# Buffer pairs re-laid and taken in another order, x and ctx loaded over 128 partitions, two transposes ahead of a copy

## The chip, the core and the metric

The kernel runs on one core of a Trainium2 chip. The metric is the device time of one execution in microseconds (us); the text gives the median of several. TensorE is called PE, VectorE DVE, ScalarE ACT, GpSimd POOL. SP is the engine whose queue issues nearly all loads here. It issues them one after the other: a load whose buffer is not yet free holds up every load behind it.

## The reference

One layer of a diffusion transformer: 512 latent tokens and 256 context tokens of 1024 numbers each.

```python
h = modulate(rms_norm(x, p['norm_pre_mix']), sh_m, sc_m)       # shift and scale come from c @ w_ada
u, q, k, v, ga, gb = split_in(h @ p['w_in'])                    # and the same for ctx
ya = s5_mixer(uc, u, p)                                         # state-space branch, scan over the tokens
yb = diff_attention(q, concat(kc, k), concat(vc, v), ...)
x  = x + g_m * rms_norm(merge_branches(ya, yb, ga, gb, p), p['norm_post_mix'])   # ends in "@ p['w_out']"
h  = modulate(rms_norm(x, p['norm_pre_ffn']), sh_f, sc_f)
...
aff = softmax(h @ w_router)                                     # expert choice: each of 16 experts
gates, idx = top_k(aff.T, cap)                                  # takes its 64 best tokens
hid = silu(xs @ w_gate) * (xs @ w_up)                           # 1024 -> 2048, per expert
ys  = hid @ w_down                                              # 2048 -> 1024, weighted, added back
x   = x + g_f * rms_norm(f, p['norm_post_ffn'])
```

Each expert has three float32 matrices of 8 MB, 24 MB in all; the sixteen experts have 384 MB. (MB is 2^20 bytes here, KB 2^10; the GB/s of the profile count 10^9.)

## The kernel before, in words

The whole program is written out, in an order fixed by hand; each engine runs its instructions in that order and waits by semaphores for what it needs.

**Start (lines 200 to 400).** x comes in as two tiles `xs` of 128 partitions by two tokens. A generator `quarters` cuts each tile into four loads of 32 partitions, issued from SP and ACT in turn; ctx is a third such tile, four loads from SP. SP then loads a part of w_in (`wu`, 512 KB) and half of what the shift and scale need of w_ada (`wa`, eight loads of 512 KB). POOL loads small parameter rows into `tmp0`. ACT takes the squares of the tokens (`squares`, four of 128x1024, after an activation table load and one Silu for `csz`). DVE makes 1/rms of them (`rx`), and multiplies the identity with it into diagonals (`dgs`), so that the matmul `xs^T dgs` (line 400) transposes and normalises at once. DVE then has a long chain for the state-space parameters (lines 330 to 345). PE meanwhile transposes parameter rows into one PSUM bank (`prmT`, line 347), DVE copies them out (line 349, after its chain), PE transposes two more pieces into the same bank (line 352), and then come the matmuls of `wa` (`ada_half`, line 369), the sums of their parts (`adaT`, line 376) and shift and scale themselves (`mod`, DVE, lines 379 to 382). Everything that follows needs `mod`.

**Buffers.** Large tiles have 128 partitions by 2048 numbers (1 MB). Each has a tag: U0 to U11 lie in a pool `up`, L0 to L7 in a pool `regs`. A queue `E` holds the free tags; `take` takes its first, `give` puts a tag back at the end.

**Output matmuls (lines 1508 to 1545).** Four token tiles of 128, eight k-tiles of w_out (`wo`, one 1 MB tile each), 24 matmuls per half row. The weights `wo` and the inputs `mp` lie in U tags. After the fourth tile, `upper.close()` frees the pool `up` as a whole, and a pool `pairs` of six 2 MB tiles P0 to P5 takes its place. They hold expert weights.

**Experts (lines 1600 to 1700).** A weight matrix is loaded in four steps of 2 MB (`load_w`). `room` decides where: the first tag in E, if it is a pair (P0 to P5, or ("SR", 0)), takes the step as one load of 2 MB; otherwise two half tiles of 1 MB are joined, the first tag and the next one in E that is no pair. Half tiles are the L tags, ("U2", 0), ("SR", 1) and ("gm", 0). After its step is issued, a tag goes back to the end of E (`done_w`), except ("U2", 0) and ("gm", 0), which serve once. So E is a ring, and its order fixes which step lands where:

```python
    def is_pair(tag):
        return tag[0] == "P" or tag == ("SR", 0)
...
        tags = [tag, next(x for x in E if not is_pair(x))]
```

`gm` holds a row that the output stage still multiplies with (DVE, line 1503). An expert's PE work is gate (64 matmul records), up (64), a transpose of the result, and down (64, `yd`); between them stand the gather of the next pair of experts' tokens and the scatter of the last. `x1` (line 1396) is a later reload of x and still uses `quarters`.

Of the kernel before, what the change touches and what calls it, by code (L numbers as in the profile page):

```python
# [9 lines left out]
F32 = mybir.dt.float32  # L10
# [3 lines left out]
OP = mybir.AluOpType  # L14
# [19 lines left out]
def layer(ctx: ExitStack, tc: tile.TileContext, A, out):  # L34
    nc = tc.nc
    PE, V, S, GP, DMA = nc.tensor, nc.vector, nc.scalar, nc.gpsimd, nc.sync
# [4 lines left out]
    up = upper.enter_context(tc.tile_pool(name="up", bufs=1))  # L41
# [5 lines left out]
    ctx.enter_context(tc.manual_schedule())  # L47


    E = deque(f"{z}{i}" for i, z in enumerate("ULUUUUULLLLUUUULLLUU"))  # L50
    tag_of, held = {}, {}

    def take(name, late=False):

        tag = E.pop() if late else E.popleft()
        t = (up if tag[0] == "U" else regs).tile([128, 2048], F32, name=name, tag=tag)
# [3 lines left out]
    def give(*ts):  # L60
        for t in ts:
            E.append(tag_of.pop(id(t)))
            held.pop(id(t))

    def big(tag, name):
        return regs.tile([128, dict(SR=6208, U2=3072)[tag]], F32, name=name, tag=tag)
# [46 lines left out]
    def row(ap, k):  # L113
        return ap.rearrange("o (k p) -> (o k) p", p=128)
# [4 lines left out]
    def quarters(ap, s):  # L119

        for q in (0, 2, 1, 3):
            yield slice(32 * q, 32 * q + 32), bass.AP(tensor=ap.tensor, offset=ap.offset + (256 * s + 2 * q) * D,
                                                      ap=[[8 * D, 32], [1, 2 * D]])

    def rsqrt_steps(o, a, get):
        sh = list(a.shape)
        i, h, t = get(*sh, dt=I32), get(*sh), get(*sh)
        V.tensor_scalar(i, a.bitcast(I32), 1, None, op0=OP.arith_shift_right)
        V.tensor_scalar(o.bitcast(I32), i, -1.0, float(0x5f3759df), op0=OP.mult, op1=OP.add)
        V.tensor_scalar(h, a, -0.5, None, op0=OP.mult)  # L130
        yield
        for _ in range(3):
            V.tensor_tensor(t, o, o, op=OP.mult)
            V.tensor_tensor(t, t, h, op=OP.mult)
            yield
            V.scalar_tensor_tensor(o, t, 1.5, o, op0=OP.add, op1=OP.mult)
# [13 lines left out]
    def rstd_of(ss, n, name):  # L150

        get = named(name)
        m, r = get(*ss.shape), get(*ss.shape)
        V.tensor_scalar(m, ss, 1.0 / n, EPS, op0=OP.mult, op1=OP.add)
        rsqrt(r, m, get)
        return r
# [20 lines left out]
    ident = keep.tile([128, 128], F32, name="ident")  # L177
# [24 lines left out]
    xs_ = [xsb[:, 2048 * s:2048 * s + 2048] for s in range(3)]  # L202
# [2 lines left out]
    S.dma_start(out=xlr[:, 0], in_=A["s5_lam_re"][0].rearrange("d g p -> (d g) p"))  # L205
    S.dma_start(out=xlr[:, 1], in_=A["s5_lam_im"][0].rearrange("d g p -> (d g) p"))
    for i in range(2):
        for n, (P, src) in enumerate(quarters(A["x"], i)):
            (DMA, S)[n % 2].dma_start(out=xs_[i][P], in_=src)
    GP.dma_start(out=prc[0:8], in_=row(A["c"], 8))  # L210
    GP.dma_start(out=prc[8:16], in_=A["c_ctx"].rearrange("(k p) -> k p", p=128))
    GP.dma_start(out=prm[0:8], in_=row(A["norm_pre_mix"], 8))
# [10 lines left out]
    def ada_load(f):  # L223

        ws = []
        for c in range(4):
            t = take("wa")
            tv = t.rearrange("p (k s f) -> p k s f", k=2, s=2)
            for s in range(2):
                c0 = 1024 * s + 512 * f  # L230
                DMA.dma_start(out=tv[:, :, s], in_=w_ada[256 * c:256 * c + 256, c0:c0 + 512].rearrange("(k p) f -> p k f", p=128))
            ws.append((t, tv))
        return ws
# [23 lines left out]
    fetch(wur[1], 0, 1)  # L257
    for i, (n, v) in enumerate((("s5_b_re", 0), ("s5_b_im", 0), ("s5_c_re", 1), ("s5_c_im", 1))):
        DMA.dma_start(out=xbc[64 * (i % 2):64 * (i % 2) + 64, v], in_=A[n][0].rearrange("d g a b -> (d g) (a b)"))
    for P, src in quarters(A["ctx"], 0):  # L260
        DMA.dma_start(out=xs_[2][P], in_=src)
    wa.append(ada_load(1))
    for p in range(2, 4):
        fetch(wur[p], 0, p)
# [6 lines left out]
    V.tensor_tensor(sum4.rearrange("p (s v) -> p s v", s=2), ide[:, 0], ide[:, 1], op=OP.add)  # L271
    early = Carve(big("U2", "early"))
    dgs = [early(128, 128) for _ in range(6)]
    hf = [early(128, 512) for _ in range(3)]


# [17 lines left out]
    pp = bank("prcT")  # L294
# [24 lines left out]
    def diagonals(i0, n, name):  # L319
        r = rstd_of(ss[:, i0:i0 + n], D, name)  # L320
        for i in range(n):
            V.tensor_scalar(dgs[i0 + i], ident, r[:, i:i + 1], None, op0=OP.mult)

    squares(range(4))
    S.activation(sc, th, AF.Sin)
# [20 lines left out]
    pp = bank("prmT")  # L346
    PE.transpose(pp[:, 0:65], prm, ident[0:65, 0:65])
    prmT = keep.tile([128, 65], F32, name="prmT")
    V.tensor_copy(prmT, pp[:, 0:65])

    for k in range(2):
        PE.transpose(pp[:, 128 + 12 * k:140 + 12 * k], prf[:, k::2], ident[0:12, 0:12])
    prfT = keep.tile([128, 3, 8], F32, name="prfT")
    V.tensor_copy(prfT.rearrange("p v (u k) -> p k v u", k=2), pp[:, 128:152].rearrange("p (k v u) -> p k v u", k=2, v=3))

# [345 lines left out]
    SR = big("SR", "SR").rearrange("p (c r g) -> p c r g", r=2, g=16)  # L701
# [655 lines left out]
    gm = gm_[:, 0:D]  # L1357
# [48 lines left out]
    yp_, oh, sgm = u_(128, 2, D), u_(128, 4, 2, CAP), u_(128, 512)  # L1406
    junk = oh.rearrange("p i e s -> p (i e s)")
    hx_ = take("hfT")
    E.extend((("SR", 0), ("U2", 0), ("SR", 1)))
    lg, aff = (keep.tile([128, 4, NE], F32, name=n) for n in ("lg", "aff"))  # L1410
    wr = keep.tile([128, 128], F32, name="wr", tag="sqj").rearrange("p (d e) -> p d e", d=8)
    cst = keep.tile([128, NE], F32, name="cst")
# [142 lines left out]
    give(*wo, *mp_[0], *mp_[1])  # L1555
    E = deque(t for t in E if isinstance(t, tuple) or t[0] != "U")
    upper.close()
    pr = ctx.enter_context(tc.tile_pool(name="pairs", bufs=1))
    E.extend(("P", i) for i in (5, 0, 1, 2, 3, 4))
    E.append(("gm", 0))  # L1560

    soft(slice(2, 4), hx_)
    rg = Carve(hx_[:, 160:])
# [190 lines left out]
    for j in range(3):  # L1754
        n = H[j].stop - H[j].start
# [30 lines left out]
    r = keep.tile([128, 4], F32, name="rl")  # L1786
# [55 lines left out]
```

## Time and profile before

| | |
|---|---|
| median of three runs | 1598.24 us (1596.92 to 1599.09) |
| time of the profiled execution | 1594.39 us, of which its span is 1592.6 us |
| PE, DVE, ACT, POOL busy in the span | 87%, 35%, 18%, 11% |
| read from HBM | 461.66 MB (10^6), 291 GB/s over the span |
| the chain that ended last, by engine | PE 54%, DMA 24%, DVE 17%, ACT 3% |

The profile records one execution. "Busy" adds the instructions of an engine; what an engine waits for stands in brackets behind an instruction, as [idle us <- who ended it]. "SPq" and "ACTq" rows are issues of loads, not the transfers. A profile's own time is a little below the median of the runs here, and sums are made against it.

### The profile page before, as it was taken

The numbers are of one execution on the slowest core, as the hardware profiler recorded it, in microseconds if no ns is written. First come the engines' busy times: TensorE is split into PE (matmuls) and PEld (weight loads), VectorE is DVE, ScalarE is ACT, GpSimd is POOL, SyncE is SP. The second block draws the span as 40 slices with busy tenths as digits, with TensorE's granted clock in tenths as the row PEclk, the third lists the DMA queues.
The fourth block names the chain that finished last, engine by engine and source line by source line (L and its number), as shares of the span: only waits on it lengthen the run. The fifth ranks groups of instructions, "written<-read, shape, count | busy, mean of one in ns | idle before, by whom it ended". The sixth has DMA issues, their size and how long they took to land.

```text
span 1592.6 us, 17729 instructions
## 1 busy us (share of the span) xinstructions
PE 1386.1 (87%) x7230; PEld 747.2 (47%) x7230; DVE 550.8 (35%) x1363; ACT 292.6 (18%) x566; POOL 173.0 (11%) x115
## 2 busy tenths in 40 slices
PE   2989959996997896799999989979989879989984
PEld 1778747884664675334334324324324324324322
DVE  4789972357556646211112102002012002112103
ACT  2473203245443322100000000000000000000002
POOL 2123212444115200000000000000000000000003
PEclk9999979998998897899999999999999999999998
DMA  9211602222553164799999999999999999999994
GB/s 285 88 38 54 122 27 87 90 67 75 183 204 120 55 238 194 288 426 427 410 427 427 426 428 428 427 427 428 427 427 426 427 427 427 427 427 426 427 412 156
DMA packets 77026, 467.01 MB, mean 293 GB/s; under 512 B 13861, under 2 KB 33505, under 8 KB 46577
## 3 DMA queue, kind: packets, MB, share of 16 engines
q1 hardware_dynamic: 75712, 463.63, 72.4%
q10 hardware_dynamic: 816, 2.13, 0.5%
q8 instruction: 57, 0.93, 0.2%
q0 software_dynamic: 416, 0.12, 0.1%
q14 instruction: 25, 0.20, 0.0%
HBM read 461.66 MB, written 2.10 MB: 291 GB/s over the span
## 4 chain that ended last, share of the span: by engine, by line
PE 54%; DMA 24%; DVE 17%; ACT 3%; issue 2%; POOL 0%; DVEq 0%; ACTq 0%; SPq 0%
PE gu L1667 15%; DMA we<-in_w_exp_up_dram 13%; PE yd L1699 10%; DMA we<-in_w_exp_down_dram 9%; PE gat L1637 5%; PE sca L1711 4%; PE wo L1514 3%; PE gate L670 2%; PE u L542 2%; DVE sp L747 2%; DVE SR L750 2%; PE k L1048 1%; PE proj L670 1%; PE o L1224 1%; DVE sq L748 1%
## 5 line engine op out<-in xcount | busy, mean ns | idle before, releaser
L1667 PE MATMUL gu<-we,gm 128*64 128x512 f32 x752 | 166.7, 595 | 17.1 <-DMA we<-in_w_exp_up_dram 13.6
L1678 DVE TENSOR_TENSOR hid<-hid,gu 128x512 f32<-128x512 f32 x32 | 21.9, 688 | 459.2 <-PE gu L1667 440.1
L1667 PE MATMUL gu<-we,gf 128*64 128x512 f32 x736 | 162.8, 594 | 14.3 <-DMA we<-in_w_exp_up_dram 13.2
L1699 PE MATMUL yd<-we,hid 128*64 128x512 f32 x704 | 155.7, 594 | 6.2 <-DMA we<-in_w_exp_down_dram 6.1
L1752 POOL TENSOR_TENSOR fin<-facc,gf 128x256 f32<-128x256 f32 (+1 forms) x12 | 10.6, 910 | 1000.3 <-DMA we<-in_w_exp_down_dram 996.1
L1667 PEld LDWEIGHTS gu<-we,gm 128*64 128x64 f32 x752 | 52.9, 137 | 129.3 <-issue 104.5
L1667 PEld LDWEIGHTS gu<-we,gf 128*64 128x64 f32 x736 | 51.6, 137 | 123.8 <-issue 100.7
L670 PE MATMUL gate<-hh,wsp 128*128 128x512 f32 x384 | 97.2, 407 | 12.4 <-ACT sg L684 12.0
L1699 PEld LDWEIGHTS yd<-we,hid 128*64 128x64 f32 x704 | 49.8, 137 | 105.0 <-issue 94.4
L1704 DVE COPY mo<-yd 64x512 f32<-64x512 f32 x15 | 10.4, 693 | 223.9 <-ACT mo L1703 223.9
L670 PEld LDWEIGHTS gate<-hh,wsp 128*128 128x128 f32 x384 | 72.9, 195 | 29.5 <-ACT sg L684 12.4
L1637 PE MATMUL gat<-mo,x 128*128 128x128 f32 x512 | 76.4, 313 | 10.2 <-DVE mo L1629 10.2
L1637 PEld LDWEIGHTS gat<-mo,x 128*128 128x128 f32 x512 | 71.8, 220 | 18.5 <-issue 15.2
L1675 ACT ACTIVATE hid<-gu 128x512 f32<-128x512 f32 x32 | 19.1, 597 | 292.2 <-PE gu L1667 292.2
L1711 PE MATMUL sca<-mo,gm 128*128 128x512 f32 (+1 forms) x136 | 61.6, 591 | 4.8 <-ACT mo L1703 4.8
L1683 ACT COPY hid<-ht 128x512 f32<-128x512 f32 x16 | 9.4, 587 | 254.1 <-PE ht L1682 254.1
L1514 PE MATMUL wo<-wo,mp 128*128 128x512 f32 x192 | 47.4, 404 | 2.4 <-DVE at L1374 2.4
L1703 ACT ACTIVATE mo<-yd 64x512 f32<-64x512 f32 x15 | 8.9, 590 | 215.1 <-PE yd L1699 215.1
L1716 DVE TENSOR_TENSOR facc<-facc,sca 128x512 f32<-128x512 f32 (+1 forms) x60 | 38.6, 651 | 18.7 <-PE sca L1711 18.6
L1667 PE MATMUL gu<-wl,gm 128*64 128x512 f32 x200 | 44.5, 593 | 0.0
L1667 PE MATMUL gu<-wl,gf 128*64 128x512 f32 x184 | 43.4, 618 | 0.0
L1711 PEld LDWEIGHTS sca<-mo,gm 128*128 128x128 f32 x136 | 21.5, 188 | 44.4 <-DVE facc L1716 23.6
(439 smaller groups left out, 1963.3 us busy)
## 6 DMA issues: line engine op xcount, KB each, us to landing
we<-in_w_exp_up_dram SPq DMA_DIRECT2D x48, 2048.0 KB, 29.6
we<-in_w_exp_gate_dram SPq DMA_DIRECT2D x45, 2048.0 KB, 33.4
we<-in_w_exp_down_dram SPq DMA_DIRECT2D x44, 2048.0 KB, 25.2
wl<-in_w_exp_gate_dram SPq DMA_DIRECT2D x9, 2048.0 KB, 28.9
araw<-in_w_ada_dram SPq DMA_DIRECT2D x16, 1024.0 KB, 6.0
wl<-in_w_exp_down_dram SPq DMA_DIRECT2D x7, 2048.0 KB, 33.1
wl<-in_w_exp_up_dram SPq DMA_DIRECT2D x7, 2048.0 KB, 26.5
wh<-in_w_exp_gate_dram SPq DMA_DIRECT2D x10, 1024.0 KB, 24.4
```

Source lines behind the costliest of these rows:

```text
L542: PE.matmul(ps, tok(a, i, kt), w[b][:, kt % 2], start=kt == first and n == 0, stop=kt == last and n == 2)
L670: PE.matmul(ps, w[:, a, kt], x[b][kt], start=kt == 0 and n == 0, stop=kt == last and n == 2)
L747: V.tensor_tensor(sp, h0, AR, op=OP.mult)
L750: V.tensor_tensor(h1, sp, sq, op=OP.add)
L1514: PE.matmul(po[j], mparts(a, kt)[:, 128 * i:128 * i + 128], wo[kt][:, D * b + 512 * j:D * b + 512 * j + 512].bitcast(F32R), start=kt == 0 ...
L1637: PE.matmul(pg, x1[i][:, nb(d)], oh[:, i].rearrange("p e s -> p (e s)"), start=i == 0, stop=i == 3)
L1667: PE.matmul(pq[b][64 * j:64 * j + 64], xst[e // 2 % 2][:, kt, e % 2], wv[:, c:c + 512], start=kt == 0, stop=kt == 7, skip_group_check=True)
L1675: S.activation(hid[0][:, 1 - e % 2, b], pq[b], AF.Silu)
L1678: V.tensor_tensor(act, act, pgu[1][b], op=OP.mult)
L1699: PE.matmul(py[64 * j:64 * j + 64], hT_[:, b, i, 64 * jf:64 * jf + 64], wv[:, c:c + 512], start=(q == 0 and i == 0), stop=(q == 3 and i == ...
L1711: PE.matmul(po, gm[:, g0:g0 + 128], yp_[:, ep % 2, c], start=True, stop=True)
L1716: V.tensor_tensor(dst, dst, po, op=OP.add)
```

## The change

Three edits. (1) The first tags in E keep their pattern of U and L but get other numbers; a `place` tile for each of U0 to U11 fixes that U0 and U1 lie under the first pair, U2 and U3 under the second, and so on, so that the two `wo` tiles of k-tiles 0 and 1 share a pair, those of 2 and 3 the next, and the `mp` tiles the last. In the ring of the experts, ("SR", 1) no longer stands ahead of the pairs but behind them, and the pairs are taken as 0, 1, 4, 2, 3, 5. (2) x and ctx are loaded as one 1 MB load for each tile, 128 partitions by two consecutive tokens; the diagonal puts the tokens into the order that the four loads gave (`turned`). (3) The copy of `prmT` stands behind the two transposes of `prf`.

```diff
-    E = deque(f"{z}{i}" for i, z in enumerate("ULUUUUULLLLUUUULLLUU"))
+    E = deque("U6 L0 U0 U7 U10 U3 U11 L1 L2 L3 L4 U8 U1 U9 U5 L5 L6 L7 U4 U2".split())
+    for k in range(12):
+        up.tile([128, 2048], F32, name="place", tag=f"U{k}")
...
+    def pairs_of(ap, s):
+
+        return ap.rearrange("o (s p i) f -> s p (o i f)", p=128, i=2)[s]
...
     for i in range(2):
-        for n, (P, src) in enumerate(quarters(A["x"], i)):
-            (DMA, S)[n % 2].dma_start(out=xs_[i][P], in_=src)
+        (DMA, S)[i].dma_start(out=xs_[i], in_=pairs_of(A["x"], i))
...
-    for P, src in quarters(A["ctx"], 0):
-        DMA.dma_start(out=xs_[2][P], in_=src)
+    DMA.dma_start(out=xs_[2], in_=pairs_of(A["ctx"], 0))
...
+    turned = ident.rearrange("p (c q) -> p q c", q=4)
...
-            V.tensor_scalar(dgs[i0 + i], ident, r[:, i:i + 1], None, op0=OP.mult)
+            V.tensor_scalar(dgs[i0 + i].rearrange("p (q c) -> p q c", q=4), turned, r[:, i:i + 1], None, op0=OP.mult)
...
-    V.tensor_copy(prmT, pp[:, 0:65])
 
     for k in range(2):
         PE.transpose(pp[:, 128 + 12 * k:140 + 12 * k], prf[:, k::2], ident[0:12, 0:12])
+    V.tensor_copy(prmT, pp[:, 0:65])
...
-    E.extend((("SR", 0), ("U2", 0), ("SR", 1)))
+    E.extend((("SR", 0), ("U2", 0)))
...
-    E.extend(("P", i) for i in (5, 0, 1, 2, 3, 4))
-    E.append(("gm", 0))
+    E.extend(("P", i) for i in (0, 1, 4, 2, 3, 5))
+    E.extend((("SR", 1), ("gm", 0)))
```

What it moves on SP's queue, at the loads for expert 0. `wh` are half tiles in L tags, `wl` is the SR region (128x4096 is its pair, 128x2048 its half, the tag ("SR", 1)), `we` are the pairs. In brackets stand the semaphores that a load waits for: DMAHW are landings of earlier loads from SP and ACT, DMASW from POOL; PE, DVE and Activation are work of these engines. Before:

```order
L1620 DMA wl_4944<-in_w_exp_gate_dram 128x2048 [waits DMAHW5_49]
L1620 DMA gm_4245<-in_w_exp_gate_dram 128x2048 [waits DMAHW6_49,DVE_49]
L1617 DMA we_5050<-in_w_exp_up_dram 128x4096 [waits DMASW4_49,DMASW5_49,DMASW3_49,DMASW6_49,DMASW2_49,DMASW7_49,DMASW1_49,DMAHW7_49,DMASW0_49,PE_49]
L1617 DMA we_5060<-in_w_exp_up_dram 128x4096 [waits DMAHW0_49]
L1617 DMA we_5070<-in_w_exp_up_dram 128x4096 [waits DMAHW1_49]
L1617 DMA we_5080<-in_w_exp_up_dram 128x4096 [waits DMAHW2_49]
L1617 DMA we_5105<-in_w_exp_down_dram 128x4096 [waits DMAHW3_49]
L1617 DMA we_5115<-in_w_exp_down_dram 128x4096 [waits DMAHW4_49]
L1620 DMA wh_5125<-in_w_exp_down_dram 128x2048 [waits DVE_49,DMAHW5_49,PE_49,Activation_49]
L1620 DMA wh_5126<-in_w_exp_down_dram 128x2048 [waits DMAHW6_49,PE_49]
L1620 DMA wh_5137<-in_w_exp_down_dram 128x2048 [waits DMAHW7_49,PE_49]
L1620 DMA wl_4944<-in_w_exp_down_dram 128x2048 [waits DMAHW0_49,PE_49]
```

And now, from the load that stands at the same place (the last 2 MB of expert 0's gate) to the second use of the same half:

```order
L1623 DMA we_5032<-in_w_exp_gate_dram 128x4096 [waits DMASW4_49,DMASW5_49,DMASW3_49,DMASW6_49,DMASW2_49,DMASW7_49,DMASW1_49,DMAHW4_49,DMASW0_49,PE_49]
L1623 DMA we_5053<-in_w_exp_up_dram 128x4096 [waits DMAHW5_49]
L1623 DMA we_5063<-in_w_exp_up_dram 128x4096 [waits DMAHW6_49]
L1623 DMA we_5073<-in_w_exp_up_dram 128x4096 [waits DMAHW7_49]
L1623 DMA we_5083<-in_w_exp_up_dram 128x4096 [waits DMAHW0_49]
L1623 DMA we_5108<-in_w_exp_down_dram 128x4096 [waits DMAHW1_49]
L1626 DMA wl_4947<-in_w_exp_down_dram 128x2048 [waits DMAHW2_49]
L1626 DMA gm_4248<-in_w_exp_down_dram 128x2048 [waits DMAHW3_49,DVE_49]
L1626 DMA wh_5128<-in_w_exp_down_dram 128x2048 [waits DVE_49,DMAHW4_49,PE_49,Activation_49]
L1626 DMA wh_5129<-in_w_exp_down_dram 128x2048 [waits DMAHW5_49,PE_49]
L1626 DMA wh_5140<-in_w_exp_down_dram 128x2048 [waits DMAHW6_49,PE_49]
L1626 DMA wl_4947<-in_w_exp_down_dram 128x2048 [waits DMAHW7_49,DMAHW2_49,PE_49]
```

The half `wl` was used for expert 0's gate and then for the end of its down matrix; now it is used twice within that down matrix, for its second step and again for its end. In both programs the first pair loaded carries the wait on PE, and the five behind it wait for landings alone.

On PE, at the start, `prmT` is the PSUM bank, `ada` the product with w_ada. Before:

```order
L295 MATMUL prcT_163<-ident_78,tmp0_91 128x16 [waits DMASW1_49,DMASW0_49,Pool_49]
L347 MATMUL prmT_252<-ident_78,tmp0_91 128x65 [waits DMASW4_49,DMASW5_49,DMASW3_49,DMASW2_49]
L352 MATMUL prmT_252<-ident_78,tmp0_91 128x12 [waits DMASW7_49,DMASW6_49,DVE_49]
L352 MATMUL prmT_252<-ident_78,tmp0_91 128x12
L369 MATMUL ada_261<-wa_122,csz_157 32x512 [waits DMAHW4_49,Activation_49]
```

And now:

```order
L301 MATMUL prcT_166<-ident_90,tmp0_103 128x16 [waits DMASW1_49,DMASW0_49,Pool_49]
L353 MATMUL prmT_255<-ident_90,tmp0_103 128x65 [waits DMASW4_49,DMASW5_49,DMASW3_49,DMASW2_49]
L357 MATMUL prmT_255<-ident_90,tmp0_103 128x12 [waits DMASW7_49,DMASW6_49]
L357 MATMUL prmT_255<-ident_90,tmp0_103 128x12
L375 MATMUL ada_264<-wa_128,csz_160 32x512 [waits DMAHW6_49,Activation_49]
```

PE's order is the same; the wait of the third transpose on DVE (its copy of `prmT`) is gone, and the matmuls of `wa` behind it wait for their own loads and for `csz`.

On ACT, at the start: its loads, the table, the Silu and the first squares. Before:

```order
L209 DMA xs_95<-in_x_dram 32x2048 x2
L209 DMA xs_95<-in_x_dram 32x2048 [waits DMAHW0_49]
L209 DMA xs_95<-in_x_dram 32x2048 [waits DMAHW2_49]
L296 ACT_TABLE_LOAD [waits DVE_49]
L296 ACTIVATE csz_157<-prcT_163 128x8x2 [waits PE_49]
L317 ACTIVATE tmp0_91,ss_191<-xs_95 128x1024 [waits DMAHW5_49,DMAHW6_49,DMAHW4_49,DMAHW1_49]
```

And now:

```order
L214 DMA xs_107<-in_x_dram 128x2048
L302 ACT_TABLE_LOAD [waits DVE_49]
L302 ACTIVATE csz_160<-prcT_166 128x8x2 [waits PE_49]
L323 ACTIVATE tmp0_103,ss_194<-xs_107 128x1024 [waits DMAHW1_49]
L323 ACTIVATE tmp0_103,ss_194<-xs_107 128x1024 [waits Activation_49]
```

Four issues became one, two of which waited for landings of earlier loads; the first square waits for one load in place of four. The DVE's and POOL's instructions are the same in kind and order.

## Rows read from the trace of the kernel before

**Rows 1.** Page, part 2: GB/s moved in 40 equal slices of the span.

```profile
GB/s 285 88 38 54 122 27 87 90 67 75 183 204 120 55 238 194 288 426 427 410 427 427 426 428 428 427 427 428 427 427 426 427 427 427 427 427 426 427 412 156
```

**Rows 2.** Stretches: start and end, length, busy by engine, granted clock, DMA, GB/s.

```profile
658.00:670.00 12.00, 12.00 (x67) 5.93 (x68) 0.82 (x2) 2.20 (x3) 0.00 (x0) 1.00 0.08 34
...
756.00:796.00 40.00, 39.31 (x164) 12.71 (x160) 6.86 (x10) 1.78 (x3) 0.00 (x0) 1.00 0.98 410
796.00:1150.00 354.00, 330.12 (x1510) 129.71 (x1508) 52.18 (x114) 20.31 (x37) 0.00 (x0) 0.98 1.01 427
1150.00:1560.00 410.00, 364.49 (x1650) 136.83 (x1652) 56.59 (x125) 24.18 (x43) 0.00 (x0) 0.98 1.01 424
```

**Rows 3.** Timeline of SP's queue: start, length, issues, loads for expert 0.

```profile
572.35 0.33 SPq L1620 DMA_DIRECT2D wl<-in_w_exp_gate_dram  x1
617.32 0.33 SPq L1620 DMA_DIRECT2D gm<-in_w_exp_gate_dram  x1
618.33 2.20 SPq L1617 DMA_DIRECT2D we<-in_w_exp_up_dram  x4
...
645.48 9.54 SPq L1620 DMA_DIRECT2D wh<-in_w_exp_down_dram  x3
669.73 0.33 SPq L1620 DMA_DIRECT2D wl<-in_w_exp_down_dram  x1
```

**Rows 4.** Timeline of PE: the last output matmuls, and three pieces of expert 0.

```profile
614.04 1.64 PE L1514 MATMUL wo<-wo,mp 128*128 128x512 f32 x6
...
667.75 1.94 PE L1667 MATMUL gu<-wl,gf 128*64 128x512 f32 x8
...
686.67 7.09 PE L1699 MATMUL yd<-we,hid 128*64 128x512 f32 x32
```

**Rows 5.** Timeline of PE late in the experts, and at the last weights.

```profile
1174.77 3.65 PE L1667 MATMUL gu<-we,gf 128*64 128x512 f32 x16 [1.33 <-DMA we<-in_w_exp_up_dram]
...
1559.00 1.95 PE L1771 MATMUL yd<-we,hid 128*64 128x256 f32 x16 [0.86 <-DMA we<-in_w_exp_down_dram]
```

**Rows 6.** Timeline of PE at the start of the span.

```profile
7.30 0.26 PE L295 MATMUL prcT<-ident,tmp 16*128 16x16 f32 x1 [7.30 <-DMA tmp<-in_c_ctx_dram]
...
27.84 0.41 PE L352 MATMUL prmT<-ident,tmp 12*128 12x12 f32 x2 [15.91 <-DVE prmT L349]
28.18 5.22 PE L369 MATMUL ada<-wa,csz 128*32 128x512 f32 x32
```

**Rows 7.** Timeline of DVE at the start of the span.

```profile
15.52 0.17 DVE L154 TENSOR_SCALAR rx<-ss 128x4 f32<-128x4 f32 x1 [5.63 <-ACT tmp L317]
...
20.09 0.88 DVE L322 TENSOR_SCALAR early<-ident,rx 128x128 f32<-128x128 f32 x4
...
27.57 0.21 DVE L349 COPY prmT<-prmT 128x65 f32<-128x65 f32 x1
...
35.22 0.25 DVE L379 TENSOR_TENSOR mod<-adaT,prmT 128x8 f32<-128x8 f32 x2 [6.75 <-PE adaT L376]
```

**Rows 8.** Timeline of ACT at the start of the span.

```profile
2.62 4.63 ACTq L209 DMA_DIRECT2D xs<-in_x_dram  x4
7.34 1.28 ACT L296 ACT_TABLE_LOAD   x1 [7.34 <-DVE rowt L301]
...
9.70 1.06 ACT L317 ACTIVATE tmp<-xs 128x1024 f32<-128x1024 f32 x1 [0.88 <-DMA xs<-in_x_dram]
...
10.88 1.06 ACT L317 ACTIVATE tmp<-xs 128x1024 f32<-128x1024 f32 x1
```

**Rows 9.** Stretches at the start, columns as in rows 2.

```profile
0.00:12.00 12.00, 0.60 (x2) 0.36 (x2) 5.59 (x33) 3.73 (x6) 7.13 (x18) 1.00 0.87 190
12.00:24.00 12.00, 0.00 (x0) 0.00 (x0) 7.72 (x31) 3.48 (x7) 2.34 (x1) 1.00 1.05 369
```

**Rows 10.** DMA issues: count, size, median us from issue to landing.

```profile
gm<-in_w_exp_gate_dram SPq DMA_DIRECT2D x1, 1024.0 KB, 5.7
```

**Rows 11.** Timeline of SP's queue: its first issues in the span.

```profile
0.74 3.83 SPq L209 DMA_DIRECT2D xs<-in_x_dram  x4
```

## The prediction

> **What bounds the kernel now.** I read the page first, for the rates in 40 slices: from the eighteenth slice, 677 us, to nearly the end the loads run at 426 to 428 GB/s, but for one slice of 410 and the last two [rows 1]. That is a rate that does not follow the work on it, so in the experts the loads are the bound. Second, the stretches: 427 GB/s from 796 to 1150 us and 424 up to 1560, where the last weights are in [rows 2]. PE is busy for 90% of that time, but does it set the end? The timeline of PE says no: late in the stage each 2 MB of matmuls stands behind a short wait for a load, and so does the last piece of expert 15 [rows 5]. So the end of the kernel is the moment from which the loads run without a gap, plus what is then left to load, divided by 427 GB/s, plus a tail.
>
> When does the gapless stretch start? Third view, SP's queue beside PE. SP loads 7 MB ahead (three `wh`, `mo`, the SR pair, the SR half) and stops at 572.35 us; the next load, into `gm`, waits until DVE has used `gm` for the last time, 617.32. Then 13 MB go out at once (1 for `gm`, 12 in pairs), three halves follow from 645.48, and SP stops again, until 669.73, at the half tile that gate's k-tile 6 is still to be read from [rows 3, 4]. From 658 to 670 us the DMA engines move 34 GB/s, that is nothing [rows 2]. At 669.73 the queue is released and does not run dry again, but for the slice of 410. So **669.73 us, a load behind PE's read of one half tile, sets the end**; 23 MB are loaded by then, 361 MB are not. The idle time up to 617 us costs nothing, since a later stop follows it.
>
> Up to 645 us the engines work one behind the other and the loads are hidden, with one place worth a look: the start. PE's two transposes wait 15.91 us for DVE's copy, which DVE reaches only at 27.57 behind its own chain; the `wa` matmuls follow at 28.18 and `mod` at 35.22 [rows 6, 7].
>
> **The change, part by part.**
>
> *The ring of buffers.* Count the loads of expert 0 in the new order: 4 MB in halves, 2 in the SR pair, six pairs of 12, then the SR half and `gm` (2), three halves (3): 23 MB again, and again the next load is the last half of the down matrix, into the SR half. But this half now holds the first MB of down's second step, not gate's k-tile 6. It comes free not in gate but after 24 of the first 32 matmul records of `yd`. In the trace those 32 start at 686.67 and take 7.09 us [rows 4]; 24 of them end at 686.67 + 5.32 = 691.99. Before, the reads of the half ended at 667.75 + 1.94 = 669.69 and SP issued 0.04 later, so the new release is 692.03: **22.3 us later**. Behind that load stand the SR pair and the six pair loads of expert 1's gate and up, 14 MB, all in free buffers. PE waits for the first of them, but not at once: it has expert 0's down left, and expert 1's gate follows. PE's own times up to that point don't change, for all it reads there is in by then. Since the loads set the end, these 22.3 us count whole, less the slice of 410: its missing 17 GB/s of 427 over 40 us are 1.6 us, in which before SP had filled every buffer and had to wait for PE. With the loads 22 us further behind PE, no buffer is full there, and the 1.6 us go. Net **+20.7 us**. Bounds: 22.3 if that gap stays, 19 if further small gaps close (424 against 427 over 410 us is 2.9, of which half can be the ramp at the end).
>
> *Pairs under the output tiles.* The pair loads now stand ahead of `gm`, so the first goes out with the end of the last output matmul, 614.04 + 1.64 = 615.68, not at 618.33: 2.65 us earlier. It still waits for that last matmul, whatever lies under it, and the other five wait for nothing more. I price it at nothing: the stop at 692 us hides it. If that stop were gone, it would be worth at most 2.65, less the 2.5 us of one MB (1.05 of 10^6 bytes at 427 GB/s) that is no longer loaded ahead at 572.35.
>
> Here a rule of the Trainium skill can be weighed. The row says that the DMA engines stood at 34 GB/s after all early loads were in [rows 2]. "DMA: Bandwidth & Descriptors", in "Rules for kernel authors", says to issue a DMA early and wait on it late. By that rule alone this edit would gain its 2.65 us; by the row it gains nothing, because what was loaded earlier only waits longer for the same stop.
>
> *x in one load per tile.* Before, ACT's four issues end at 2.62 + 4.63 = 7.25, the table load follows at 7.34 for 1.28 us, and the first square starts at 9.70 when x is in [rows 8]. Now one issue is left on ACT; with about 0.6 us the table load ends at about 4.5, and ACT next needs PE's first transpose, 7.30 + 0.26 [rows 6]. Is x in? The trace has a 1 MB load over 128 partitions into idle engines, and it landed 5.7 us after its issue [rows 10]: 0.74 + 5.7 is 6.4 for the first tile (SP's first issue was at 0.74 [rows 11] and still is), 2.62 + 5.7 = 8.3 for the second, later by some sharing. So four squares of 1.18 each (9.70 to 10.88 [rows 8]) run from about 7.8 to 12.6, where DVE's `rx` began at 15.52: **2.9 us** earlier for DVE's chain, if the small loads that PE's transpose needs are no later; 0 if they or x are 3 us later. The diagonals read the identity with a step; four take 0.88 us [rows 7]; between no change and twice that, I take no change. For ctx SP saves three issues; the u matmuls that PE still has to do cover it, so nothing; without them it would be worth what x is.
>
> *The transposes.* PE no longer waits for DVE at 27.84. The `wa` matmuls then follow their loads. x, `wu` and `wa` are 6.5 MB or 6.8 of 10^6 bytes; at the 369 GB/s of the stretch from 12 to 24 us they take 18.5 us [rows 9], from about 2 us on, so the last lands at 20.5. The last quarter of the `wa` matmuls, 5.22 / 4, ends at 21.8; from the end of `ada` to `mod` took 35.22 - 33.40 = 1.8 us, so `mod` could start at 23.6. DVE is not there yet: its copy of `prmT` comes at 27.57 - 2.9 = 24.7, a second small copy at 24.9, so `mod` starts at 25.1. That is 10.1 us before 35.22. Without the 2.9 us of x it is 28.4, and 6.8 us. I take **9.0**, near the upper end, since x has more than a microsecond to spare, and 1 us for small loads that may land later beside x. All work up to the experts follows from `mod` engine by engine, and the later loads of the front go out as these engines free their buffers, so I carry the 9.0 us to the experts unchanged.
>
> *Sum.* 22.3 - 1.6 - 9.0 = +11.7 us. The profiled execution took 1594.39 us (span 1592.6 and 1.8 around it): 1606.1 for its like. The median of the runs shown, 1598.24, is 3.85 above it, which I add: **1609.9, say 1610 us**, 0.7% slower. About 0.2%, 3.2 us, is what a measurement of this kernel can tell from no change.
>
> **The rivals.**
>
> *PE, not the loads, ends the experts (faster).* Then a later release is hidden behind PE's backlog and only the start counts: 1598.2 - 9.0 = 1589. For it: PE is busy 90% of the time, and up to about 1150 us it hardly waits. Against: from there to the end it does wait for loads, at the last weights too [rows 5], with the rate flat [rows 2]. It decides at the loads of expert 1: the stop would have to cost less than the 10.6 us that the start and the closed gap give. Chance 5%.
>
> *The early issue pays (faster).* If the last half of down were not held up, the loads would start 2.65 us earlier and nothing be lost: 1598.2 - 9.0 - 2.7 = 1586.5. Against: the half's second use stands in the new order, and a load can't overwrite what PE has still to read. Chance 2%. The rule of the Trainium skill's page weighed above ("DMA: Bandwidth & Descriptors", "Rules for kernel authors") points this way.
>
> *The start gains little (slower).* The `wa` loads or the small rows land no sooner, or DVE's chain doesn't move: 6.8 us or less; with the +20.7, 1612 to 1617, and 1619 with nothing. For it: the first 12 us move only 190 GB/s [rows 9], and why is not settled by a row. Against: the wait of 15.91 us is certainly gone. Chance 17%.
>
> *Each pair is released by its own two tiles.* That is what the layout is for, and the order shows it not done. Even then the stop at the half stays, and the time is that of the forecast; no chance of its own.
>
> **How the numbers follow.** The forecast has 76%, the start that gains little 17, the two faster ones 7. Faster by over 0.2% is then 7%. Within 0.2% (up to +3.2) would need a start of 17 us or a stop of under 14: 3%, out of the forecast's share. Slower: 90%. The range: at the low end the sum with the upper start and the closed small gaps, 19 - 10.1 = +9, and some microseconds that the list of gaps may miss, so 1604; at the high end 22.3 - 6.8 = +15.5, and a little of the weak start, 1617. That leaves the faster rivals and a start of nothing outside, with under 2 in 10.
>
> **What would show it.** Right: SP's second load of expert 0's down into the SR half goes out behind `yd`, some 22 us of added DMA idle time after about 650 us; the rate is 427 GB/s from there without the slice of 410; the waits of PE for weights begin hundreds of us earlier; `mod` starts near 26 us, with `ada` done before DVE is free; the output matmuls end about 9 us earlier. Wrong: `mod` at 30 or later; the end of the experts not moved with the release; PE later in expert 0 than 9 us before its old times.

## The result, and the profile after

The changed kernel takes 1611.94 us (median of four, 1610.17 to 1614.82) where the kernel before took 1598.66 beside it (median of four, 1596.92 to 1599.48): the ratio is 1.0086, with a 95% interval of 1.0069 to 1.0104. It is slower by about 13 us, and by 16 us against the median of 23 later executions of the kernel before, 1595.56 us. The profiled execution took 1610.17 us, its span is 1608.4 us, 15.8 more than before. Two things happened, as the prediction had them: the front became faster, and SP stopped longer in expert 0. The front reached the experts 4.9 us earlier and the end came 15.8 us later, so the stop cost 20.7 us, about four times what the front gained.

The loads per slice, to be laid beside [rows 1]. Page of the changed kernel, GB/s in 40 slices of 40.2 us:

```profile
GB/s 331 38 54 83 76 27 96 92 92 86 154 181 157 34 190 318 127 373 426 426 427 427 426 427 428 425 427 427 427 427 426 427 426 427 428 427 428 426 413 159
```

Where one slice of 288 led to the plateau, there now stand 318, 127 and 373: the loads have started and stopped again. The slice of 410 is gone. The stretches, columns as in [rows 2]:

```profile
645.00:684.00 39.00, 38.87 (x196) 16.37 (x194) 3.30 (x6) 4.87 (x8) 0.00 (x0) 1.00 0.28 114
...
690.00:756.00 66.00, 57.19 (x280) 24.02 (x278) 8.66 (x25) 4.20 (x8) 0.00 (x0) 0.97 1.01 428
756.00:796.00 40.00, 39.31 (x163) 12.78 (x160) 7.01 (x11) 1.78 (x3) 0.00 (x0) 1.00 1.01 427
```

SP's queue in the changed kernel, where [rows 3] showed the loads for expert 0 before:

```profile
611.77 0.33 SPq L1623 DMA_DIRECT2D we<-in_w_exp_gate_dram  x1
612.15 2.16 SPq L1623 DMA_DIRECT2D we<-in_w_exp_up_dram  x4
...
640.27 9.84 SPq L1626 DMA_DIRECT2D wh<-in_w_exp_down_dram  x3
687.18 0.33 SPq L1626 DMA_DIRECT2D wl<-in_w_exp_down_dram  x1
687.56 0.42 SPq L1623 DMA_DIRECT2D wl<-in_w_exp_gate_dram  x1
688.03 1.81 SPq L1623 DMA_DIRECT2D we<-in_w_exp_gate_dram  x3
689.88 1.49 SPq L1623 DMA_DIRECT2D we<-in_w_exp_up_dram  x3
```

The stop now ends at 687.18 instead of 669.73, and the seven loads behind it, 14 MB, then go out in 4 us: their buffers had long been free. PE beside it, where [rows 4] stood:

```profile
610.10 1.64 PE L1520 MATMUL wo<-wo,mp 128*128 128x512 f32 x6
...
644.80 1.94 PE L1673 MATMUL gu<-wh,gf 128*64 128x512 f32 x8
...
681.77 3.65 PE L1705 MATMUL yd<-we,hid 128*64 128x512 f32 x16
685.25 1.89 PE L1705 MATMUL yd<-wl,hid 128*64 128x512 f32 x8
...
712.98 3.65 PE L1673 MATMUL gu<-we,gf 128*64 128x512 f32 x16 [1.58 <-DMA we<-in_w_exp_gate_dram]
717.82 3.65 PE L1673 MATMUL gu<-we,gf 128*64 128x512 f32 x16 [1.18 <-DMA we<-in_w_exp_up_dram]
```

The reads of the half in down end at 685.25 + 1.89 = 687.14, and SP issues 0.04 us later. PE waits for a weight for the first time at 712.98, in expert 1. In the kernel before the first such wait came at 942 us ([rows 5] show one at 1174). The first pair goes out at 611.77, right behind the last output matmul (610.10 + 1.64 = 611.74).

The start, where [rows 6 to 8] stood: PE, then DVE, then ACT of the changed kernel, from one view for each engine.

```profile
8.59 0.26 PE L301 MATMUL prcT<-ident,tmp 16*128 16x16 f32 x1 [8.59 <-DMA tmp<-in_c_ctx_dram]
...
22.34 1.06 PE L375 MATMUL ada<-wa,csz 128*32 128x512 f32 x6 [0.31 <-DMA wa<-in_w_ada_dram]
24.11 1.05 PE L382 MATMUL adaT<-sum,tmp 128*128 128x4 f32 x8 [0.71 <-ACT tmp L377]
27.43 2.05 PE L406 MATMUL xT<-early,xs 128*128 128x128 f32 x8 [2.27 <-DVE prfT L360]
```
```profile
14.71 0.17 DVE L160 TENSOR_SCALAR rx<-ss 128x4 f32<-128x4 f32 x1 [3.21 <-ACT tmp L323]
...
27.12 0.16 DVE L360 COPY prfT<-prmT 128x24 f32<-128x24 f32 x1
27.30 0.25 DVE L385 TENSOR_TENSOR mod<-adaT,prmT 128x8 f32<-128x8 f32 x2
```
```profile
8.97 1.05 ACT L323 ACTIVATE tmp<-xs 128x1024 f32<-128x1024 f32 x1
...
12.35 1.06 ACT L323 ACTIVATE tmp<-xs 128x1024 f32<-128x1024 f32 x1 [1.06 <-DMA xs<-in_x_dram]
```

`mod` starts at 27.30 instead of 35.22, 7.9 us earlier, and now PE waits for DVE (2.27 us before `xT`), not DVE for PE. What `xT` waits for is not `mod`: it reads only x and the diagonals, and in the kernel before too it starts (35.04) ahead of `mod` (35.22); the scaling behind it, on ACT, is what reads `mod`. By the kernel's text `xT` takes the PSUM bank that `prmT` had, so it has to wait for DVE's last copy out of that bank, `prfT`. No run gives it another bank. Expert 0's gate starts at 644.80, which is only 4.9 us before its 649.71 in the kernel before. The rest of the 7.9 us is lost within 30 us of `mod`, and the granted clock shows where. The stretch from 24 to 36 us, columns as in [rows 2] (the clock is the third number from the right), before and then changed:

```profile
24.00:36.00 12.00, 7.44 (x50) 3.33 (x50) 3.97 (x21) 0.60 (x1) 0.00 (x0) 1.00 1.04 266
```
```profile
24.00:36.00 12.00, 9.63 (x55) 8.56 (x56) 6.69 (x30) 3.82 (x6) 0.96 (x1) 0.72 1.03 328
```

A granted clock of 1.00 is 2.4 GHz, 0.50 is 1.2 GHz; a stretch of 0.72 has some of either. The first eight records of `xT` take 2.05 us where they took 1.14, the first twelve of `u` 3.69 where they took 3.05. `xT` starts 7.6 us earlier than before; by 58 us 5.0 are left, and 4.9 reach the experts.

### The profile page after: what moved, and what is told of

It is laid out like the page before. It is cut to its first block, busy times and chain, and to the rows that moved or that the text cites. A ratio compares the mean times of both kernels' runs of the same rounds, so it can differ in the third digit from the quotient of the medians.

```text
span 1608.4 us, 17710 instructions
## 1 busy us (share of the span) xinstructions
PE 1394.9 (87%) x7230; PEld 745.4 (46%) x7230; DVE 553.9 (34%) x1363; ACT 292.6 (18%) x566; POOL 173.9 (11%) x115
## 4 chain that ended last, share of the span: by engine, by line
PE 47%; DMA 30%; DVE 17%; ACT 3%; issue 2%; POOL 0%; SPq 0%; DVEq 0%; ACTq 0%
DMA we<-in_w_exp_up_dram 18%; DMA we<-in_w_exp_down_dram 11%; PE gu L1673 11%; PE yd L1705 8%; PE gat L1643 4%; PE sca L1717 4%; PE wo L1520 3%; PE gate L676 2%; DVE SR L756 2%; PE u L548 2%; DVE sp L753 1%; PE k L1054 1%; PE proj L676 1%; DVE sq L754 1%; PE y L877 1%
## 5 line engine op out<-in xcount | busy, mean ns | idle before, releaser
L1673 PE MATMUL gu<-we,gf 128*64 128x512 f32 x752 | 169.1, 600 | 22.8 <-DMA we<-in_w_exp_up_dram 18.3
L1643 PE MATMUL gat<-mo,x 128*128 128x128 f32 x512 | 71.8, 300 | 10.2 <-DVE mo L1635 10.2
L1643 PEld LDWEIGHTS gat<-mo,x 128*128 128x128 f32 x512 | 67.3, 208 | 18.3 <-issue 15.2
L1520 PEld LDWEIGHTS wo<-wo,mp 128*128 128x128 f32 x192 | 36.6, 194 | 10.4 <-DVE at L1380 2.8
```

Of the source, the lines that this page charges most:

```text
L1520: PE.matmul(po[j], mparts(a, kt)[:, 128 * i:128 * i + 128], wo[kt][:, D * b + 512 * j:D * b + 512 * j + 512].bitcast(F32R), start=kt == 0 ...
L1643: PE.matmul(pg, x1[i][:, nb(d)], oh[:, i].rearrange("p e s -> p (e s)"), start=i == 0, stop=i == 3)
L1673: PE.matmul(pq[b][64 * j:64 * j + 64], xst[e // 2 % 2][:, kt, e % 2], wv[:, c:c + 512], start=kt == 0, stop=kt == 7, skip_group_check=True)
```

## The experiments

The theory: the end of the kernel is SP's last stop plus a fixed time, since the loads run without a gap from there; the front shifts PE and so the stops with it; the stop moved because of where the SR half stands in the ring. Rivals: the pair layout or order costs the time; PE or full buffers hide a moved stop; the start's gain is lost on the way. The first four runs test the ring, the others the start. Ratios are to the kernel before, with their 95% intervals; the time of a run's profile is its span.

**The ring as it was, the rest as changed.**

```diff
-    E.extend((("SR", 0), ("U2", 0)))
+    E.extend((("SR", 0), ("U2", 0), ("SR", 1)))
...
-    E.extend((("SR", 1), ("gm", 0)))
+    E.append(("gm", 0))
```

> The changed kernel with one line of the ring put back: ("SR", 1) ahead of the pairs again; layout, pair order, loads of x and transposes as changed. If the use of the half sets the end: its release goes back behind gate's k-tile 6, which the whole front now reaches 4.9 us earlier (expert 0's gate at 644.80 instead of 649.71), so 669.73 - 4.9 = 664.8; the end moves with it, 1594.4 - 4.9 = 1589.5 us in the profile, 0.3% faster than before. If instead the layout or the pair order has cost the time, it stays near 1610. If what the start gains is lost again on the way to the end, 1594.

Measured: 0.9959 (0.9945 to 0.9973), median 1589.73 us, span 1588.2. Of the changed kernel's loss nothing is left, and the front's gain comes out at the end. SP's queue of this run, the second load of the half, and a later stop, which I come back to below:

```profile
666.58 0.33 SPq L1626 DMA_DIRECT2D wl<-in_w_exp_down_dram  x1
...
752.10 3.76 SPq L1623 DMA_DIRECT2D we<-in_w_exp_up_dram  x2
767.51 10.63 SPq L1623 DMA_DIRECT2D we<-in_w_exp_down_dram  x4
```

The release is 20.6 us before that of the changed kernel. It is 1.8 later than expected, because this execution's front was 1.7 later than that of the changed kernel's profile (gate at 646.46).

**Only the half moved, the rest as before.**

```diff
-    E.extend((("SR", 0), ("U2", 0), ("SR", 1)))
+    E.extend((("SR", 0), ("U2", 0)))
...
-    E.append(("gm", 0))
+    E.extend((("SR", 1), ("gm", 0)))
```

> The kernel before with ("SR", 1) moved behind the pairs and nothing else. If the release of that half sets the end: SP's second load of it waits until 692.0 instead of 669.73, the slice of 410 GB/s closes, and the end is 22.3 - 1.6 = 20.7 us later: 1615.1 us in the profile, 1.3% slower. If PE hid the later load, no more than a few us; if the pair layout is the cause, no change (1594).

Measured: 1.0138 (1.0120 to 1.0156), median 1618.29 us; the profiled execution, at the upper end of its runs (1615.38 to 1620.78), has a span of 1619.0.

```profile
697.63 0.33 SPq L1620 DMA_DIRECT2D wl<-in_w_exp_down_dram  x1
```

The release stands at 697.63, not 692.0; but in this execution PE's `slot` transposes start at 649.93 where they started at 644.48 before, so the front was 5.4 late, and 692.0 + 5.4 = 697.4. Less these 5.4 us the span is 21.0 us longer than before, where 20.7 was expected. Moving this one entry of the ring behind the pairs costs 22.7 us of median (19 to 25 by the interval). The theory holds, PE does not hide it, and the layout is not needed for it.

**Only the layout and the order of the pairs.**

```diff
-    E = deque(f"{z}{i}" for i, z in enumerate("ULUUUUULLLLUUUULLLUU"))
+    E = deque("U6 L0 U0 U7 U10 U3 U11 L1 L2 L3 L4 U8 U1 U9 U5 L5 L6 L7 U4 U2".split())
+    for k in range(12):
+        up.tile([128, 2048], F32, name="place", tag=f"U{k}")
...
-    E.extend(("P", i) for i in (5, 0, 1, 2, 3, 4))
+    E.extend(("P", i) for i in (0, 1, 4, 2, 3, 5))
```

> The kernel before with the new tags and places of U and L and the pair order 0, 1, 4, 2, 3, 5, but ("SR", 1) still ahead of the pairs. If where a pair lies does not matter, since the first pair waits for the last output matmul anyway and a later stop follows: within 1.5 us of 1594.4 in the profile. If pairs come free one by one, their loads go out during the output matmuls, well before 615 us; if that paid, 1592 or less.

Measured: 0.9998 (0.9987 to 1.0009), median 1594.90 us: no change. Its profiled execution is the longest of its twelve (span 1598.1); the front was 5 us late in it. Here `gm` still stands ahead of the pairs, so this run can't show a pair going out during the output matmuls; the changed kernel could, and its first pair waits for the last of them.

**The half that comes free first, as the last of expert 0's loads.** The changed kernel with another ring:

```diff
+    h0, h1, h2 = (x for x in E if isinstance(x, str))
+    E = deque((h0, h1, ("SR", 1), ("SR", 0), ("U2", 0), h2))
     E.extend(("P", i) for i in (0, 1, 4, 2, 3, 5))
-    E.extend((("SR", 1), ("gm", 0)))
+    E.append(("gm", 0))
```

> The changed kernel with a ring in which the half that is used again first is the one read third in expert 0's gate (half, half, SR half, SR pair, U2, half, pairs, gm). Then SP's last load of expert 0's down is released behind gate's k-tile 2, 644.80 + 3 x 1.95 = 650.7, the SR pair behind k-tile 5 at 656.5, the first pair of expert 1 behind up's k-tile 1 at 664.3, and 28 MB instead of 23 are in at 669.2: 0.5 + 5 x 2.456 = 12.8 us ahead of before. If the loads set the end through the time from which they run without a gap: 1594.4 - 12.8 = 1581.6 us, 1580 to 1586 with some new gaps where SP finds every buffer full. If PE or full buffers bind as soon as the loads are further ahead, no better than the start alone: 1589.5.

Measured: 0.9978 (0.9967 to 0.9989), median 1592.51 us, span 1591.6: no better than with the ring as it was, and the expected 12.8 us are not there. Two steps of this expectation were wrong. SP's queue of this run:

```profile
656.65 0.33 SPq L1628 DMA_DIRECT2D wl<-in_w_exp_down_dram  x1
665.67 0.33 SPq L1625 DMA_DIRECT2D wl<-in_w_exp_gate_dram  x1
673.83 7.20 SPq L1625 DMA_DIRECT2D we<-in_w_exp_gate_dram  x3
...
755.67 3.76 SPq L1625 DMA_DIRECT2D we<-in_w_exp_up_dram  x2
771.08 7.20 SPq L1625 DMA_DIRECT2D we<-in_w_exp_down_dram  x3
```

And PE of the same run at the start of gate:

```profile
648.66 1.94 PE L1675 MATMUL gu<-wh,gf 128*64 128x512 f32 x8
650.52 1.21 PE L1645 MATMUL gat<-mo,x 128*128 128x128 f32 x8
651.66 1.94 PE L1675 MATMUL gu<-wh,gf 128*64 128x512 f32 x8
```

First, I had taken 1.95 us for a k-tile of expert 0's gate. Between two of them stands a piece of the gather (`gat`, 1.21), so one comes every 3.0 us, and the buffers behind the half come free later: the SR pair at 665.67, the first pair at 673.83. By then 26 MB are loaded, and 673.83 less the 3 MB more at 2.46 us each is 666.5: as good as the stop at 666.58 above, with a front 2.2 us later (gate 648.66 against 646.46). Of the 12.8 us, 4.9 were the front's; of the 7.9 that the ring itself was to bring, 2.3 were there. Second, these are taken back later. The stretch of this run in which expert 2 begins:

```profile
756.00:796.00 40.00, 39.20 (x165) 12.94 (x161) 7.60 (x11) 1.92 (x4) 0.00 (x0) 1.00 0.93 386
```

386 GB/s, where the kernel before had 410 and the run with the old ring 423. SP's own wait is no longer than in the other two: it has issued two pair loads by 755.67 + 3.76 = 759.43, and issues the next at 771.08, 11.65 us on, as from 760.46 to 772.11 in the kernel before and from 755.86 to 767.51 with the old ring. But here the loads are further ahead, so that nearly all that SP has issued is in before PE frees the next pair: from 770 to 772 us the DMA engines move 8 GB/s. It is this last stop that the end follows. From it to the end of the span the kernel before takes 1592.6 - 772.11 = 820.5 us, this run 1591.6 - 771.08 = 820.5, the run with the old ring 1588.2 - 767.51 = 820.7; in the six other runs with the half ahead of the pairs it is 820.4 to 820.9. The row of the kernel before:

```profile
756.70 3.76 SPq L1617 DMA_DIRECT2D we<-in_w_exp_up_dram  x2
772.11 7.19 SPq L1617 DMA_DIRECT2D we<-in_w_exp_down_dram  x3
```

In the changed kernel this stop costs nothing, and the end is counted from the one in expert 0: 1608.4 - 687.18 = 921.2 us, and 1619.0 - 697.63 = 921.4 with the half moved alone. The Trainium skill, "DMA: Bandwidth & Descriptors", "Rules for kernel authors", advises to issue a DMA early and to wait on it late, so that its fixed setup cost overlaps with compute. In this run the earlier issue gained nothing at the end, since the 2.3 us won in expert 0 were paid back at the next full buffer.

**The transposes alone.** The third edit put into the kernel before.

```diff
-    V.tensor_copy(prmT, pp[:, 0:65])
     for k in range(2):
         PE.transpose(pp[:, 128 + 12 * k:140 + 12 * k], prf[:, k::2], ident[0:12, 0:12])
+    V.tensor_copy(prmT, pp[:, 0:65])
```

> The kernel before with the two transposes ahead of the copy and nothing else. DVE's copy stays near 27.6, so mod starts near 28.1 instead of 35.22, 7.1 us earlier. PE then stands idle for some 3 us between the sums of ada and the first xT. If that idle time is what brings the granted clock down to 0.50 in the changed kernel (some 2.6 us lost up to 58 us), it comes down here too: expert 0's gate 4 to 5 us earlier and the end with it, 1589.5 to 1590.5 us in the profile. If the loads of x in one piece have to do with it, the clock stays at 1.00 and 7 us come through: 1587.5.

Measured: 0.9962 (0.9948 to 0.9977), median 1589.93 us, span 1588.7; expert 0's gate at 645.42, 4.3 us earlier. DVE, PE and the clock of this run:

```profile
29.05 0.24 DVE L379 TENSOR_TENSOR mod<-adaT,prmT 128x8 f32<-128x8 f32 x2 [1.48 <-PE adaT L376]
```
```profile
26.19 1.06 PE L369 MATMUL ada<-wa,csz 128*32 128x512 f32 x6 [0.31 <-DMA wa<-in_w_ada_dram]
27.95 1.06 PE L376 MATMUL adaT<-sum,tmp 128*128 128x4 f32 x8 [0.71 <-ACT tmp L371]
```
```profile
32.00:34.00 2.00, 2.00 (x8) 1.74 (x8) 0.90 (x6) 0.98 (x2) 0.00 (x0) 0.50 1.05 244
```

`mod` is 6.2 us earlier, not 7.1, since `wa`, which SP issues behind its four loads of x, lands last here. The clock falls to 0.50 here too. So x in one piece is not needed for it; but neither is the long idle time before `xT`, which this run doesn't have.

**The loads alone.** The second edit put into the kernel before (the load of ctx and the turned diagonal with it).

```diff
-        for n, (P, src) in enumerate(quarters(A["x"], i)):
-            (DMA, S)[n % 2].dma_start(out=xs_[i][P], in_=src)
+        (DMA, S)[i].dma_start(out=xs_[i], in_=pairs_of(A["x"], i))
```

> The kernel before with x and ctx loaded in one piece for each tile, and the diagonal turned, and nothing else. DVE's rx 0.8 us earlier, as in the changed kernel (15.52 to 14.71); the transposes still wait for the copy and the copy for DVE's chain: mod 0.6 us earlier, the end between 0 and 1 us earlier, 1593.8 us in the profile, which the measurement can't tell from no change. The small loads of POOL (c_ctx, 7.30) land about 1.3 us later and the second x tile after 12 us, if x in one piece is the cause of both. If neither moves, x is in by 8.3 and rx starts 2.9 us earlier, as the prediction had it.

Measured: 0.9996 (0.9985 to 1.0007), median 1594.73 us: no change. PE and ACT of this run:

```profile
8.71 0.26 PE L299 MATMUL prcT<-ident,tmp 16*128 16x16 f32 x1 [8.71 <-DMA tmp<-in_c_ctx_dram]
...
27.35 0.41 PE L356 MATMUL prmT<-ident,tmp 12*128 12x12 f32 x2 [14.95 <-DVE prmT L353]
```
```profile
12.49 1.06 ACT L321 ACTIVATE tmp<-xs 128x1024 f32<-128x1024 f32 x1 [1.08 <-DMA xs<-in_x_dram]
```

Both late landings of the changed kernel are here too: PE has c_ctx at 8.71 instead of 7.30, and ACT waits for the second tile of x until 12.49.

**PE kept busy before `xT`.** The changed kernel with the old ring, and eight matmuls that nobody reads, behind the sums of `ada` (`spare` is the PSUM bank of `ada`, which ACT has copied out by then):

```diff
+    for _ in range(8):
+        PE.matmul(spare[:, 0:128], ident, ident, start=True, stop=True, skip_group_check=True)
```

> The changed kernel with ("SR", 1) ahead of the pairs (1588.2 us span) and eight matmuls more, of the identity with itself, which nobody reads, between the sums of ada and the first xT, where PE was idle from 24.9 to 27.5. If that idle time is what brings the granted clock down: the clock stays at 1.00 from 24 to 36 us, xT and u run as before the change, expert 0's gate is 2.6 us earlier and the end with it, a span of 1585.6. If the thin stretch of ada matmuls before it has already brought it down, the clock still falls to 0.50 and the span stays at 1588 to 1589.

```profile
24.00:36.00 12.00, 11.16 (x84) 9.83 (x85) 8.60 (x34) 5.24 (x8) 2.38 (x1) 1.00 1.03 322
```

The clock stays at 1.00, and the first twelve records of `u` end at 33.5 instead of 36.8 us in the run with the old ring. At the end it is not to be seen: 0.9954 (0.9938 to 0.9970), median 1589.44 us, span 1588.9. In its profiled execution PE is 3.8 us ahead of that run at the first output matmul (559.25 against 563.06) and 0.2 ahead at the last `affT` (625.12 against 625.31). Between them some `wo`, `hfT` and `lg` matmuls take longer than they did there (single `hfT` 0.42 against 0.28), at a granted clock of 0.79 from 558 to 566 us and 0.80 from 610 to 618, where that run had 1.00 in both. The start gave more than the 2.6 expected, and other matmuls in this execution lost it; by the medians no gain is shown.

**x ahead of the other loads on SP, with five and with eight of these matmuls.**

```diff
-        (DMA, S)[i].dma_start(out=xs_[i], in_=pairs_of(A["x"], i))
+        DMA.dma_start(out=xs_[i], in_=pairs_of(A["x"], i))
```

> As the run with eight matmuls more, but five, and both tiles of x issued by SP, ahead of its wu and wa loads. If the second tile was late because it shared the engines with wa: the third square no longer waits for it (1.06 us), rx and mod are 1.1 us earlier, and the end with them, a span of 1584.5. If it is late for another reason, no difference to the run with eight.

> The run with both tiles of x on SP, with eight more matmuls in place of five (16 records, 2.03 us at the full clock). With eight and x as changed, the granted clock stayed at 1.00 from 24 to 36 us; with five and x first it fell to 0.50 although PE was not idle from 24.2 on. If the number of these matmuls is what counts: the clock stays at 1.00, xT starts at 27.2, u runs as in the run with eight, and the span is 1583 to 1585 where the clock from 480 to 570 us is as good as in the run with five (1584.5). If the one run that kept the clock was chance: it falls again, the eight take some 3.5 us, xT starts at 28.5, and the span is 1586 or more.

Measured: 0.9946 (0.9932 to 0.9961), median 1587.23 us and span 1584.5 with five; 0.9944 (0.9927 to 0.9962), 1586.87 and 1584.8 with eight. The stretch from 24 to 36 us, with five and then with eight:

```profile
24.00:36.00 12.00, 11.56 (x77) 10.36 (x78) 7.46 (x27) 5.21 (x8) 2.38 (x1) 0.86 1.03 338
```
```profile
24.00:36.00 12.00, 11.70 (x87) 10.28 (x88) 8.63 (x31) 5.18 (x7) 2.38 (x1) 1.00 1.03 341
```

The third square no longer waits for x in either run (with five it starts at 11.68 instead of 12.35). `rx` starts at 14.04 with five and at 14.41 with eight instead of 14.71, 0.7 and 0.3 us earlier, not 1.1, since c_ctx is later still (8.96 and 9.33). SP also issues the second tile earlier than ACT did, at 1.2 instead of 2.85, and with five it lands 8.4 us after its issue instead of 9.4. So its place ahead of `wa` shortened the load by 1.0 us and the earlier issue brought 1.6; that sharing with `wa` alone made the tile late is not shown. The Trainium skill, "DMA: Bandwidth & Descriptors", "Queues, rings and completion order", says that a DMA engine takes turns between the queues that have work for it; the 9.4 us of the second tile on ACT's queue beside SP's loads, against 8.4 ahead of them on SP's, agree with that, though no run here shows the turns themselves. With eight matmuls the clock stayed at 1.00 in both runs that had them; with five it fell to 0.50 from 26 to 28 us although PE had been busy since 24.2. The last two runs beat both kernels, the one before by 8 to 9 us and the changed one by about 25; how much of that is due to x and how much to the matmuls, the intervals don't separate from the run with the old ring.

## Why the prediction was right, and where it was not

**The stop in expert 0** was right in place and size. Predicted: 692.03 on the old front, behind 24 of the first 32 `yd`. Measured: 687.18, and with the 4.9 us of the front 692.1. The run with the half alone shows the price at the end, the run without it the price taken away.

**The slice of 410 closes** was right: from SP's release to the end of the span 921.2 us where it took 922.9, 1.7 us for the 1.6 of the sum. But the prediction called 669.73 the stop that sets the end of the kernel before. Strictly it is the one at 772.11, to which that slice belongs: the run with the earliest half shows that an earlier release in expert 0 gains nothing, because the loads then stop there. For a later release, which is what the change brings, this makes only the 1.7 us of difference that the sum had.

**The early pair loads are worth nothing** was right: the first pair waits for the last output matmul, and the layout alone changes no time.

**The start, 9.0 us, was mis-sized**; 4.9 came through. Two terms: `mod` was set at 25.1 and came at 27.30. The first square was to start at 7.8; it started at 8.97, because c_ctx, on which `csz` waits, landed 1.3 us later, the "small loads that may land later beside x" for which 1 us had been taken off. And the second tile of x, which was to be in by 8.3, was in at 12.35 and cost 1.06: its "some sharing" came to 9.4 us from issue to landing, beside the 4 MB of `wa` that SP now issues right behind its own loads. The trace of the kernel before already had the second tile late, in a row that the prediction did not use:

```profile
13.16 1.06 ACT L317 ACTIVATE tmp<-xs 128x1024 f32<-128x1024 f32 x1 [1.12 <-DMA xs<-in_x_dram]
```

Together that is 2.2 us, of which the forecast had allowed for 1.1 by taking 9.0 and not 10.1. Then "I carry the 9.0 us to the experts unchanged" failed: 2.6 us went to the granted clock of 0.50 between `mod` and 36 us, which no row of the kernel before showed. Two of the prediction's own signs speak to this step: PE reached expert 0 later than 9 us before its old times, which it had named as a sign of being wrong, and the output matmuls end 3.9 us earlier (611.74 against 615.68), not 9. What the loads of x in one piece add to the transposes is 0.6 us in the profile (gate at 644.80 against 645.42), which the measured times can't tell from nothing; alone they give nothing.

**The sum** was +11.7 us against +15.8 in the spans; the 4.1 us between them are the start's. That the median, 1611.94, is only 2 us from the forecast of 1610 is luck: the 3.85 us added between profile and median were too many, which made up for half of the 4.1. The changed kernel's median is 1.8 above its profile, and of 23 later runs of the kernel before the median is 1595.56, 1.2 above its profile.

**The rivals.** PE does not end the experts: moving the half alone made the span 21.0 us longer, its late front taken off, where 20.7 was forecast. The rival that the start gains little (6.8 us or less, 1612 to 1617) describes the start better than the forecast did; it and the forecast differ in size only.

What stays open: what brings the granted clock down between 24 and 36 us. It fell with PE idle before `xT` and without, and with five matmuls put in, but not in the two runs with eight. The kernel before, whose `ada` matmuls run in one piece from 28.18 on, kept 1.00, and so did the three runs that leave its transposes where they were. Open is also whether `xT` in another PSUM bank would start earlier.

## What to carry to other kernels

In a ring of buffers filled by one in-order queue, count where a buffer is used for the second time: the load that waits for it holds up everything behind it, and moving one buffer behind the six pairs cost 22 us here. Look then for the last stop of the queue before the loads run for good: only what moves that stop moves the end, so releasing a buffer earlier gains until the next stop, and what moves the whole front gains in full. When a wait goes away at the start, add up again who is late next (here two loads beside each other and then PE's clock), since each of them takes its share of the gain.

## What the runs showed of the hardware that was not expected

The granted clock in the mixed work from 480 to 570 us differs from one execution to the next, and PE's way through it too. In the profile of the layout run it was 0.79 over this stretch, 0.81 before; PE was 1.1 us behind the kernel before at 432 us (`onT`) and 4.9 behind at 563 (`wo`), and the span was 5.5 longer, while the medians are equal. That the clock accounts for all of this is not shown. A single profile is no measure of a few microseconds here. Also: with x in one 1 MB load for each tile a small POOL load, issued at the same time, lands later, 6.3 and 6.4 us after its issue in the changed kernel and in the run with the loads alone instead of 5.0 (PE has c_ctx at 8.59 and 8.71 instead of 7.30). Two things changed there at once: the loads are over 128 partitions and not 32, and SP, with fewer issues of x, comes to `wu` and `wa` 6 us sooner (1.21 and 1.67 instead of 7.46 and 8.14), so that 246 instead of 176 GB/s move in the first 8 us. Which of the two delays the small load no run here shows.
